# Differential attention: gates as token-major products joined to the head output, q's norm in the exponentials' scale, the rotation moved off GpSimd

## The chip, the cores and the metric

The kernel runs on one core of one Trainium2 chip. The metric is the time of one execution on the device in microseconds; the median over repeated runs is compared. TensorE (PE in the profile) does the matrix products and the transposes, VectorE (DVE) and ScalarE (ACT) work on their results, GpSimd (POOL) does small arithmetic, and SyncE (SP) issues most of the DMAs.

## The reference

The network has four layers (differential attention, latent attention, a gated linear recurrence, differential attention again) with a per-layer embedding gate after each, and then a second part with a state space mixer and a dilated attention whose inputs are modulated by a vector `c`. There are 256 tokens and 2048 features, all in float32. What the change touches is the differential attention of layers 0 and 3, and when the modulation's weights are fetched:

```python
def diff_attention(xn, positions, w_in, q_gain, k_gain, ..., sub_gain, w_out, layer_idx):
    u = xn @ w_in
    q, k, v, gate = jnp.split(u, 4, axis=-1)
    q = rope(rms_norm(q.reshape(B, S, H, 2, d), q_gain), positions)
    k = rope(rms_norm(k.reshape(B, S, H, 2, d), k_gain), positions)
    ...
        sc = jnp.einsum('bqhcd,bkhcd->bhcqk', q[:, s:e], k[:, :e]) * scale
        pr = jax.nn.softmax(masked(sc), axis=-1)
        w = pr[:, :, 0] - lam * pr[:, :, 1]
        return jnp.einsum('bhqk,bkhe->bqhe', w, v[:, :e])
    o = rms_norm(o, sub_gain) * (1.0 - lam_init)
    y = o.reshape(B, S, DA_WIDTH) * jax.nn.silu(gate)
    return y @ w_out
```

There are 8 heads; each has two q and two k of 128 features and a v of 256. The modulation is `silu(c) @ ada_w + ada_b`, for two later layers.

## The kernel before

Every large product is made from split operands. A weight piece of four row tiles (128 rows each) by 512 columns is fetched by SyncE into one of three buffers (`load`, L282). `split` then makes from each half of it, two row tiles, a rounded copy `hi` on ScalarE (L294) and the rest `lo` on VectorE (L296), each in one of three buffers. TensorE multiplies hi by hi, hi by lo and lo by hi and adds the three. `matB` (L328) gives feature-major results: the weights are stationary, 256 tokens are streamed, 12 products for each row tile. `matA` (L350) gives token-major results: the activations are stationary, 512 weight columns are streamed, 6 products for each row tile.

Work beside that main stream is written as generators, called jobs. `ktick` counts the row tiles of the main stream, and a job that has yielded a number goes on after so many of them. The framework then orders the instructions of each engine by priority; `high_priority(offset=self.ahead)` in `chunks` moves a weight load and its split 150 places forward. Each engine runs its queue in order.

A differential attention layer (`layer_a`) goes through four groups of 512 features (two heads). For each group it makes k, q and v as token-major products, and then the gate of the group before as a feature-major product. The job `qk` sums squares (L701 on ScalarE, L702 on VectorE), forms the norm on GpSimd (`head_r`, L576 to L581, with the power at L425), scales by the norm (L707), and rotates with `rope_apply`: GpSimd multiplies by the cosines (L565), VectorE multiplies two halves by the sines (L568) and adds (L569). Then it transposes and copies (L720, L721). The job `head` makes the scores (L736, L739), maxima (L742), exponentials (L748, their bias from GpSimd's L744), weighs the two softmaxes (L756), transposes them (L760 to L764), multiplies by v (L767 to L769), squares (L773), forms its norm on GpSimd (L776 to L784), scales (L786), transposes again (L793) and writes the feature-major output under the gain (L796). `gated` multiplies the gate's product by the norm of the rows (L606; `norm_job` has broadcast it by transposes, L440, and a copy, L451), applies Silu (L609), multiplies by the head output (L610), and splits (L613, L614). The split results of all groups are the operands of the output product `out_proj`.

The modulation runs beside all this: `ada_setup` cuts its weights into 192 pieces of 512 KB (`aw`). Every piece is fetched by SyncE at L1224 into the tile `aw` of a pool with one buffer, and multiplied and added by VectorE (L1235); `bg_rate` says how many pieces go with each weight piece of the main stream.

## Time and profile before

| | us |
|---|---|
| median of 3 runs | 3432.39 |
| lowest and highest run | 3428.05, 3438.39 |
| span of the profiled execution | 3436.4 |
| TensorE busy | 3355.9 (98%) |
| VectorE busy | 2472.9 (72%) |
| ScalarE busy | 1728.2 (50%) |
| GpSimd busy | 422.8 (12%) |

The profile is of one execution whose span lies between the lowest and the highest run; its time is not listed apart from its span, and the runs leave only a few microseconds around it. Times in it are microseconds from the start of the span, unless marked ns. A busy share says how much an engine worked, not whether it was waited for; for that one reads a stretch of the span, who waits there, and for whom. The first differential attention runs up to 437 us, the second from 1529 to 1944 us.

### The profile page before, as it was taken

What the parts mean: (1) busy time and instruction counts of PE and PEld (TensorE: products, weight loads), DVE (VectorE), ACT (ScalarE), POOL (GpSimd) and SP (SyncE); (2) the same over time, 40 slices, a digit from 0 to 9 for tenths busy, and PEclk for the clock granted to TensorE, in tenths of its full rate; (3) what the DMA queues carried; (4) which work ended last, traced back from release to release, by engine and by line L of the source; (5) the groups of instructions that cost most, each with busy time, mean ns of one, the idle gap of its engine ahead of it and who ended that gap; (6) DMA issues with size and microseconds to landing.
All of it is one profiled execution on the core that took longest, in us unless ns stands there. A gap on an engine that the chain in (4) does not pass through costs nothing.

```text
span 3436.4 us, 59860 instructions
## 1 busy us (share of the span) xinstructions
PE 3355.9 (98%) x24624; PEld 3165.8 (92%) x24624; DVE 2472.9 (72%) x3441; ACT 1728.2 (50%) x2329; POOL 422.8 (12%) x620
## 2 busy tenths in 40 slices
PE   8999999999999999999999999999999998999997
PEld 6788899998899999997788999999999998898997
DVE  7767777766677776777677678768778867777566
ACT  5455445466645676544444544555556433334443
POOL 3212201132110000112222010000000001000002
PEclk9999999999999999999999999999999999999999
DMA  6556556643465555656565566454545764786442
GB/s 234 188 200 215 211 203 223 217 142 138 149 226 200 195 183 190 224 207 218 178 216 188 191 238 230 175 184 174 193 175 184 252 233 169 297 296 240 158 143 102
DMA packets 113826, 685.48 MB, mean 199 GB/s; under 512 B 13264, under 2 KB 13968, under 8 KB 47120
## 3 DMA queue, kind: packets, MB, share of 16 engines
q1 hardware_dynamic: 109152, 670.49, 54.6%
q10 hardware_dynamic: 4400, 11.18, 1.1%
q8 instruction: 192, 3.15, 0.4%
q14 instruction: 82, 0.67, 0.1%
HBM read 679.45 MB, written 2.16 MB: 198 GB/s over the span
## 4 chain that ended last, share of the span: by engine, by line
PE 81%; DVE 8%; issue 2%; POOL 2%; DMA 2%; ACT 1%; DVEq 0%; POOLq 0%
PE acc L328 59%; PE acc L350 11%; PE ps L328 4%; DVE lo L296 2%; DMA aw<-in_ada_w_dram 2%; POOL m L425 1%; DVE aacc L1235 1%; DVE t L568 1%; PE ps L1149 1%; PE ps L736 1%; PE ps L1551 1%; DVE m L702 0%; DVE t L569 0%; POOL m L576 0%; PE ps L986 0%
## 5 line engine op out<-in xcount | busy, mean ns | idle before, releaser
L294 ACT ACTIVATE hi<-w 128x1024 fp32r<-128x1024 f32 x1082 | 1140.5, 1055 | 1514.3 <-PE acc L328 982.8
L296 DVE TENSOR_TENSOR lo<-w,hi 128x1024 fp32r<-128x1024 f32 x1082 | 1354.6, 1257 | 551.3 <-ACT hi L294 545.0
L328 PE MATMUL acc<-x,hi 128*128 128x256 f32 x7168 | 1314.0, 285 | 8.5 <-DVE x L1425 3.6
L328 PEld LDWEIGHTS acc<-x,hi 128*128 128x128 f32 x7168 | 1121.4, 192 | 17.7 <-issue 6.2
L328 PE MATMUL acc<-x,lo 128*128 128x256 f32 x3584 | 1016.3, 284 | 0.2 <-DVE lo L296 0.2
L328 PE MATMUL acc<-s,hi 128*128 128x256 f32 x4864 | 882.5, 284 | 2.5 <-DVE t L938 2.4
L328 PEld LDWEIGHTS acc<-s,hi 128*128 128x128 f32 x4864 | 760.7, 192 | 2.9 <-issue 2.6
L328 PE MATMUL acc<-s,lo 128*128 128x256 f32 x2432 | 689.9, 284 | 0.5 <-DVE lo L296 0.5
L328 PEld LDWEIGHTS acc<-x,lo 128*128 128x128 f32 x3584 | 689.2, 192 | 1.1 <-DVE lo L296 0.4
L350 PE MATMUL acc<-hi,x 128*128 128x512 f32 x1920 | 603.2, 395 | 2.1 <-ACT hi L294 2.1
L328 PEld LDWEIGHTS acc<-s,lo 128*128 128x128 f32 x2432 | 467.9, 192 | 1.3 <-DVE lo L296 0.9
L350 PEld LDWEIGHTS acc<-hi,x 128*128 128x128 f32 x1920 | 358.8, 189 | 75.2 <-ACT hi L294 3.1
L350 PE MATMUL acc<-lo,x 128*128 128x512 f32 x960 | 381.1, 397 | 33.5 <-DVE lo L296 33.4
L1235 DVE SCALAR_TENSOR_TENSOR aacc<-aw,siluc,aacc 128x512 f32<-128x512 f32 x255 | 208.1, 816 | 146.9 <-DMA aw<-in_ada_w_dram 144.5
L350 PEld LDWEIGHTS acc<-lo,x 128*128 128x128 f32 x960 | 181.3, 189 | 87.9 <-DVE lo L296 49.8
L328 PE MATMUL ps<-x,hi 128*128 128x256 f32 (+1 forms) x576 | 107.7, 286 | 0.3 <-DVE x L1266 0.3
L328 PEld LDWEIGHTS ps<-x,hi 128*128 128x128 f32 (+1 forms) x576 | 88.5, 185 | 1.5 <-DVE x L1266 0.5
L1235 DVE SCALAR_TENSOR_TENSOR ssacc<-s,siluc,ssacc 128x512 f32<-128x512 f32 x105 | 78.7, 750 | 14.2 <-DMA s<-in_ada_w_dram 12.7
L405 POOL TENSOR_TENSOR ssacc<-ssacc,s 128x512 f32<-128x512 f32 x24 | 35.1, 1463 | 434.3 <-ACT s L399 434.2
L431 POOL TENSOR_SCALAR m<-m 128x2 f32<-128x2 f32 x16 | 13.2, 826 | 564.1 <-DVE m L415 534.0
L328 PE MATMUL ps<-x,lo 128*128 128x256 f32 (+1 forms) x288 | 81.2, 282 | 0.0
L425 POOL TENSOR_TENSOR m<-m,mhalf 128x4 f32<-128x4 f32 (+2 forms) x61 | 74.2, 1217 | 11.1 <-DVE m L1374 6.1
(362 smaller groups left out, 2983.4 us busy)
## 6 DMA issues: line engine op xcount, KB each, us to landing
w<-in_a_w_in_dram SPq DMA_DIRECT2D x127, 1024.0 KB, 4.8
w<-in_a_in_w_dram SPq DMA_DIRECT2D x80, 1024.0 KB, 4.8
aw<-in_ada_w_dram SPq DMA_DIRECT2D x136, 512.0 KB, 3.7
w<-in_ple_w_gate_dram SPq DMA_DIRECT2D x64, 1024.0 KB, 5.0
w<-in_kv_w_dram SPq DMA_DIRECT2D x48, 1024.0 KB, 4.8
w<-in_a_w_out_dram SPq DMA_DIRECT2D x32, 1024.0 KB, 4.8
w<-in_c_w_in_dram SPq DMA_DIRECT2D x32, 1024.0 KB, 4.9
w<-in_a_out_w_dram SPq DMA_DIRECT2D x32, 1024.0 KB, 4.8
```

The lines of the kernel that those rows point to most:

```text
L294: nc.scalar.activation(hi[:, :m], src, AF.Copy)
L296: nc.vector.tensor_tensor(out=lo[:, :m], in0=src, in1=hi[:, :m].bitcast(F32), op=ALU.subtract)
L328: self.nc.tensor.matmul(out=o, lhsT=a[:, c0:c1], rhs=b, start=(k == 0 and p == 0 and first), stop=(k == kts - 1 and p == 2 and last))
L350: self.nc.tensor.matmul(out=a[:, t, :n], lhsT=b[:, s], rhs=w, start=(k == 0 and p == 0), stop=(k == kts - 1 and p == 2))
L405: nc.gpsimd.tensor_tensor(out=acc, in0=acc, in1=f[:, :512], op=ALU.add)
L425: self.nc.gpsimd.tensor_tensor(out=out, in0=in_, in1=h, op=ALU.pow)
L431: self.nc.gpsimd.tensor_scalar(out=m, in0=m, scalar1=1.0 / dim, scalar2=eps, op0=ALU.mult, op1=ALU.add)
L568: nc.vector.tensor_tensor(out=out[:, :, a, :], in0=x[:, :, 1 - a, :], in1=s, op=ALU.mult)
L736: nc.tensor.matmul(out=scv[:, c, :], lhsT=Q[g][:, c0 + c, t * P:(t + 1) * P], rhs=K[g][:, c0 + c, :nk], start=True, stop=False)
L1149: nc.tensor.matmul(out=qs[b][:, T * i:T * i + T], lhsT=wv[:, i * P:(i + 1) * P], rhs=xv[:, k, :], start=(kk == 0 and p == 0 and i == 0), s ...
L1235: nc.vector.scalar_tensor_tensor(out=st["acc"], in0=w[:, i, :], scalar=c, in1=st["acc"], op0=ALU.mult, op1=ALU.add)
L1551: nc.tensor.matmul(out=po[64 * k:64 * k + 64, :], lhsT=tok[:, 0, 64 * hh:64 * hh + 64], rhs=ms[k][:, 0:T], start=True, stop=False)
```

## The change

In `layer_a` the gate of a group is now computed as a token-major product, between q and v of its own group, with Silu taken straight from the result by ScalarE under the norm of the rows (`SG`). The head output is scaled by its norm and by this gate in one instruction, transposed, and split under the gain into `Y`; `gated` and the broadcast of the row norm are no longer called here. The rotation is done on VectorE alone, from the product itself, before any norm. k is scaled by its norm after it, in a later step of the job; q is not scaled at all: its norm is part of the scale and the bias of the exponentials (`RQ`). Several steps of the jobs are cut by further `yield`s and their distances differ. `out_proj` takes its operands as the heads finish (`close`). In `ada_setup` the DMA and the allocation of its tile are traced under the same high priority as the weight loads. The changed file also drops comments, which moves line numbers.

```diff
-    def norm_job(self, acc):
+    def norm_job(self, acc, rb=True):
         st = {}
         def g():
             st["r"] = self.rms_r(acc(), D, EPS)
+            if not rb:
+                return
...
-        nj, nst = self.norm_job(acc)
-        K, Q, V, oT = {}, {}, {}, {}
+        nj, nst = self.norm_job(acc, rb=False)
+        K, Q, V, SG, RQ, Y = {}, {}, {}, {}, {}, {}
         self.bg_rate = 0.45
         def tables():
...
                 self.row_load(g[:, P:], "a_q_norm", P * j, P)
                 st["k"] = self.rope_tab(tabs[:, 0:2], g[:, :P], 0, 64)
                 st["q"] = self.rope_tab(tabs[:, 2:4], g[:, P:], 0, 64)
-        def qk(which, dst, g, a):
+                gs = self.rp.tile([P, 2], F32, name="gs", tag="gs", bufs=2)
+                nc.gpsimd.tensor_scalar(
+                    out=gs, in0=self.vec("a_sub_norm", 2 * j, 2), scalar1=1.0 - li, scalar2=0.0, op0=ALU.mult, op1=ALU.add)
+                st["gs"] = gs
+        def turned(which, a, t):
+            C, S = st[which]
+            x4 = a[:, t, :].rearrange("p (h a b) -> p h a b", h=4, a=2)
+            u, v = self.tmp(), self.tmp()
+            u4 = u.rearrange("p (h a b) -> p h a b", h=4, a=2)
+            v4 = v.rearrange("p (h a b) -> p h a b", h=4, a=2)
+            nc.vector.tensor_tensor(out=u4, in0=x4, in1=C[:, t].unsqueeze(1).to_broadcast([P, 4, 2, 64]), op=ALU.mult)
+            nc.vector.tensor_tensor(
+                out=v4, in0=x4[:, :, ::-1, :], in1=S[:, t].unsqueeze(1).to_broadcast([P, 4, 2, 64]), op=ALU.mult)
+            nc.vector.tensor_tensor(out=v, in0=v, in1=u, op=ALU.add)
+            return v
+        def qk(which, dst, g, a, wait):
             tables()
-            C, S = st[which]
...
             rq = self.head_r(ss, st["r2"], nst["r"], EPS, (2, 4))
-            qrs = []
-            for t in range(2):
-                qn = self.tmp()
-                nc.vector.tensor_tensor(
-                    out=qn.rearrange("p (h e) -> p h e", h=4), in0=a[:, t, :].rearrange("p (h e) -> p h e", h=4),
-                    in1=rq[:, t, :].unsqueeze(2).to_broadcast([P, 4, P]), op=ALU.mult)
-                qr = self.tmp()
-                self.rope_apply(
-                    qr.rearrange("p (h a b) -> p h a b", h=4, a=2), qn.rearrange("p (h a b) -> p h a b", h=4, a=2),
-                    C, S, t, 4, 64)
-                qrs.append(qr)
-            yield 20
+            if which == "q":
+                rs = self.rp.tile([P, 2, 2, 4], F32, name="rq", tag="rq", bufs=3)
+                nc.gpsimd.tensor_scalar(out=rs[:, 0], in0=rq, scalar1=scale, scalar2=0.0, op0=ALU.mult, op1=ALU.add)
+                nc.gpsimd.tensor_scalar(out=rs[:, 1], in0=rq, scalar1=-scale, scalar2=0.0, op0=ALU.mult, op1=ALU.add)
+                RQ[g] = rs
+            qrs = [turned(which, a, t) for t in range(2)]
+            if which == "k":
+                yield 3
+                for t in range(2):
+                    v = qrs[t].rearrange("p (h e) -> p h e", h=4)
+                    nc.vector.tensor_tensor(
+                        out=v, in0=v, in1=rq[:, t, :].unsqueeze(2).to_broadcast([P, 4, P]), op=ALU.mult)
+            yield wait
             d = self.slot()
             for t in range(2):
                 pt = self.ps()
...
                 nc.scalar.activation(d[:, :, t * P:(t + 1) * P], pt.rearrange("p (h e) -> p h e", h=4), AF.Copy)
             dst[g] = d
-        def head(h):
+        def head(h, pend, w1, w2):
             g, c0 = h // 2, 2 * (h % 2)
-            self.finish(*pend[g])
-            if g not in oT:
-                oT[g] = self.slot()
+            self.finish(*pend)
             vs = slice(T * (h % 2), T * (h % 2) + T)
             ws = []
             for t in range(2):
...
-                nc.gpsimd.tensor_scalar(out=nm, in0=mx, scalar1=-scale, scalar2=0.0, op0=ALU.mult, op1=ALU.add)
+                nc.gpsimd.tensor_tensor(out=nm, in0=mx, in1=RQ[g][:, 1, t, c0:c0 + 2], op=ALU.mult)
...
                 for c in range(2):
                     nc.scalar.activation(
-                        e[:, c, :], scv[:, c, :], AF.Exp, bias=nm[:, c:c + 1], scale=scale, accum_out=sm[:, c:c + 1])
+                        e[:, c, :], scv[:, c, :], AF.Exp, bias=nm[:, c:c + 1], scale=RQ[g][:, 0, t, c0 + c:c0 + c + 1],
+                        accum_out=sm[:, c:c + 1])
                 rs = self.small([P, 2])
                 nc.vector.reciprocal(rs, sm)
                 co = self.small([P, 1])
                 nc.gpsimd.tensor_tensor(out=co, in0=rs[:, 1:2], in1=sm[:, 0:1], op=ALU.mult)
                 nc.gpsimd.tensor_tensor(out=co, in0=co, in1=self.nlam[:, j:j + 1], op=ALU.mult)
-                w = e[:, 0, :]
-                nc.vector.scalar_tensor_tensor(out=w, in0=e[:, 1, :], scalar=co, in1=w, op0=ALU.mult, op1=ALU.add)
-                ws.append((w, rs))
-            yield 12
+                ws.append((e, co, rs))
+            yield 2
+            for e, co, _ in ws:
+                nc.vector.scalar_tensor_tensor(
+                    out=e[:, 0, :], in0=e[:, 1, :], scalar=co, in1=e[:, 0, :], op0=ALU.mult, op1=ALU.add)
+            yield w1
             pw = self.ps()
...
             wT = self.tmp(384)
             nc.scalar.activation(wT, pw[:, :384], AF.Copy)
-            yield 2
+            yield w2
             po = self.ps()
             nc.tensor.matmul(out=po[:, 0:T], lhsT=wT[:, 0:P], rhs=V[g][:, 0, vs], start=True, stop=True)
             nc.tensor.matmul(out=po[:, T:2 * T], lhsT=wT[:, P:2 * P], rhs=V[g][:, 0, vs], start=True, stop=False)
...
                 nc.scalar.activation(sq[:, t * T:(t + 1) * T], po[:, t * T:(t + 1) * T], AF.Square, accum_out=so[:, t:t + 1])
             r0 = self.small([P, 2])
             for t in range(2):
-                nc.gpsimd.tensor_copy(out=r0[:, t:t + 1], in_=ws[t][1][:, 0:1])
+                nc.gpsimd.tensor_copy(out=r0[:, t:t + 1], in_=ws[t][2][:, 0:1])
...
             ro = self.small([P, 2])
             self.rpow(ro, a)
             nc.gpsimd.tensor_tensor(out=ro, in0=ro, in1=r0, op=ALU.mult)
+            yield 3
             o = self.tmp()
             for t in range(2):
-                nc.vector.tensor_scalar(
-                    out=o[:, t * T:(t + 1) * T], in0=po[:, t * T:(t + 1) * T], scalar1=ro[:, t:t + 1], scalar2=None,
-                    op0=ALU.mult)
-            yield 6
+                nc.vector.scalar_tensor_tensor(
+                    out=o[:, t * T:(t + 1) * T], in0=po[:, t * T:(t + 1) * T], scalar=ro[:, t:t + 1],
+                    in1=SG[g][:, t, vs], op0=ALU.mult, op1=ALU.mult)
+            yield 3
             pt = self.ps()
             for e2 in range(2):
                 for t in range(2):
                     nc.tensor.transpose(
                         pt[:, e2 * T + t * P:e2 * T + (t + 1) * P], o[:, t * T + e2 * P:t * T + (e2 + 1) * P], self.ident)
+            if g not in Y:
+                Y[g] = (self.slot(F32R), self.slot(F32R))
+            hi, lo = Y[g]
             for e2 in range(2):
-                nc.vector.tensor_scalar(
-                    out=oT[g][:, c0 + e2, :], in0=pt[:, e2 * T:(e2 + 1) * T], scalar1=self.vec("a_sub_norm", 2 * j + e2),
-                    scalar2=1.0 - li, op0=ALU.mult, op1=ALU.mult)
-        y = []
-        pend, heads = {}, {}
-        def gate(g):
-            a = self.groupB(W, 16, 3 * D + 512 * g, x)
-            self.finish(*heads[g])
-            y.append(self.gated(a, nst["rb"], oT.pop(g)))
+                pv, gv = pt[:, e2 * T:(e2 + 1) * T], st["gs"][:, e2:e2 + 1]
+                nc.scalar.activation(hi[:, c0 + e2, :], pv, AF.Copy, scale=gv)
+                nc.vector.scalar_tensor_tensor(
+                    out=lo[:, c0 + e2, :], in0=pv, scalar=gv, in1=hi[:, c0 + e2, :].bitcast(F32),
+                    op0=ALU.mult, op1=ALU.subtract)
+        heads = {}
         for g in range(4):
-            kj = self.go(qk("k", K, g, self.matA(W, 16, D + 512 * g, 512, x)))
-            qj = self.go(qk("q", Q, g, self.matA(W, 16, 512 * g, 512, x)))
-            a = self.matA(W, 16, 2 * D + 512 * g, 512, x)
-            v = self.flat(self.slot()).rearrange("p (t n) -> p t n", t=2)
-            for t in range(2):
-                nc.scalar.activation(v[:, t, :], a[:, t, :], AF.Copy, scale=nst["r"][:, t:t + 1])
-            V[g] = v
-            pend[g] = (kj, qj)
             last = g == 3
-            heads[g] = [self.go(head(2 * g + i), 2 + i * (8 if last else 16)) for i in range(2)]
-            if g:
-                gate(g - 1)
-        gate(3)
-        return self.out_proj(self.W("a_w_out", j), 16, y, prep)
...
         def piece(layer, q, k):
             def f():
+                src = self.W("ada_w_2", layer).part(512 * q, 512, 2 * k, 2 * k + 2)
                 if self.late:
                     w = self.flat(self.slot()).rearrange("p (a n) -> p a n", a=2)
+                    nc.sync.dma_start(out=w, in_=src)
                 else:
-                    w = self.ap_.tile([P, 2, 512], F32, name="aw", tag="aw")
-                nc.sync.dma_start(
-                    out=w, in_=self.W("ada_w_2", layer).part(512 * q, 512, 2 * k, 2 * k + 2))
+                    with self.tc.high_priority(offset=self.ahead):
+                        w = self.ap_.tile([P, 2, 512], F32, name="aw", tag="aw")
+                        nc.sync.dma_start(out=w, in_=src)
```

How the order of the instructions moves, at three places. On VectorE, around the q product of the third group of the first layer; `acc` is the product, `t` temporaries, `m` the norm or sums, `s` tables, `aacc` the modulation's sum. Before:

```order
L702 TENSOR_REDUCE m<-t 128x4 x2
L1233 TENSOR_SCALAR aacc<-aw,siluc 128x512
L296 TENSOR_TENSOR lo<-w,hi 128x1024
L707 TENSOR_TENSOR t<-acc,m 128x512
L1235 SCALAR_TENSOR_TENSOR aacc<-aw,siluc,aacc 128x512
L568 TENSOR_TENSOR t<-t,s 128x4x64
L296 TENSOR_TENSOR lo<-w,hi 128x1024
L568 TENSOR_TENSOR t<-t,s 128x4x64
L707 TENSOR_TENSOR t<-acc,m 128x512
L569 TENSOR_TENSOR t<-t 128x512
```

The same engine and product after the change:

```order
L722 TENSOR_REDUCE m<-t 128x4 x2
L710 TENSOR_TENSOR t<-acc,s 128x512
L296 TENSOR_TENSOR lo<-w,hi 128x1024
L711 TENSOR_TENSOR t<-acc,s 128x512
L710 TENSOR_TENSOR t<-acc,s 128x512
L713 TENSOR_TENSOR t<-t 128x512
L296 TENSOR_TENSOR lo<-w,hi 128x1024
L711 TENSOR_TENSOR t<-acc,s 128x512
L1273 SCALAR_TENSOR_TENSOR aacc<-aw,siluc,aacc 128x512
L713 TENSOR_TENSOR t<-t 128x512
```

The two passes with the norm `m` (L707) are gone; the rotation reads the product and the tables, and the splits stand among its six passes.

On SyncE, in the middle of the first layer; `w` are weight pieces, `aw` the modulation's. Before:

```order
L282 DMA w<-in_a_w_in_dram 128x2048 x11
L1224 DMA aw<-in_ada_w_dram 128x1024
L282 DMA w<-in_a_w_in_dram 128x2048
L1224 DMA aw<-in_ada_w_dram 128x1024
L282 DMA w<-in_a_w_in_dram 128x2048
L1224 DMA aw<-in_ada_w_dram 128x1024
```

After:

```order
L282 DMA w<-in_a_w_in_dram 128x2048 x10
L1263 DMA aw<-in_ada_w_dram 128x1024
L282 DMA w<-in_a_w_in_dram 128x2048
L1263 DMA aw<-in_ada_w_dram 128x1024
L282 DMA w<-in_a_w_in_dram 128x2048
L1263 DMA aw<-in_ada_w_dram 128x1024
L282 DMA w<-in_a_w_in_dram 128x2048 x2
```

A piece still follows a weight load each time, with shifts of one load here and there; over the whole program both orders have 136 such pieces.

On ScalarE, in the last group of the first layer, before (Silu at L609, exponentials at L748 done earlier):

```order
L609 ACT_TABLE_LOAD
L609 ACTIVATE t<-t 128x512 x2
L294 ACTIVATE hi<-w 128x1024
L613 ACTIVATE s<-t 128x512 x2
L294 ACTIVATE hi<-w 128x1024
```

and after (Silu at L847, exponentials at L767):

```order
L847 ACT_TABLE_LOAD
L847 ACTIVATE s<-acc,r 128x512
L767 ACT_TABLE_LOAD
L767 ACTIVATE t,m<-ps,m,rq 128x128
L294 ACTIVATE hi<-w 128x1024
L767 ACTIVATE t,m<-ps,m,rq 128x128
L847 ACT_TABLE_LOAD
L847 ACTIVATE s<-acc,r 128x512
L294 ACTIVATE hi<-w 128x1024
L767 ACT_TABLE_LOAD
L767 ACTIVATE t,m<-ps,m,rq 128x256
```

Silu and the exponentials of the last two heads now alternate, with a table load at each turn; over the whole program the table loads on ScalarE go from 81 to 89.

## Rows read from the trace of the kernel before

**Rows 1.** Busy time in three stretches: stretch, length, engines, clock, DMA share
```profile
core 0: us, PE busy (x) PEld busy (x) DVE busy (x) ACT busy (x) POOL busy (x), PEclk, DMA share, GB/s
35.00:437.00 402.00, 386.63 (x2136) 330.53 (x2135) 290.61 (x390) 186.65 (x287) 89.30 (x160) 1.00 0.58 205
437.00:700.00 263.00, 262.86 (x2192) 262.35 (x2191) 187.63 (x228) 127.88 (x156) 37.99 (x54) 1.00 0.60 211
1546.00:1938.00 392.00, 378.94 (x2080) 322.72 (x2081) 278.51 (x358) 184.63 (x282) 83.68 (x154) 1.00 0.57 200
```

**Rows 2.** Waits of PE, 35 to 437: total, times, longest
```profile
PE acc L350 <- DVE lo L296: 14.2, 16, 2.0
```

**Rows 3.** The same, 1546 to 1938
```profile
PE acc L350 <- DVE lo L296: 12.7, 16, 1.8
PE ps L440 <- POOL r L425: 0.6, 1, 0.6
```

**Rows 4.** Timeline of PE, 160 to 172: a product that waited
```profile
164.46 0.50 PE L350 MATMUL acc<-lo,x 128*128 128x512 f32 x1 [1.61 <-DVE lo L296]
```

**Rows 5.** Timeline of DVE in that stretch: start, us, instruction, idle before
```profile
161.03 0.69 DVE L707 TENSOR_TENSOR t<-acc,m 128x512 f32<-128x512 f32 x1 [2.38 <-POOL m L581]
...
162.10 2.31 DVE L296 TENSOR_TENSOR lo<-w,hi 128x1024 fp32r<-128x1024 f32 x1
...
165.86 1.84 DVE L568 TENSOR_TENSOR t<-t,s 128x256 f32<-128x256 f32 x2
...
168.02 1.21 DVE L296 TENSOR_TENSOR lo<-w,hi 128x1024 fp32r<-128x1024 f32 x1
```

**Rows 6.** Timeline of GpSimd in that stretch
```profile
161.89 1.43 POOL L565 TENSOR_TENSOR t<-t,s 128x512 f32<-128x512 f32 x1 [0.90 <-DVE t L707]
165.48 1.61 POOL L565 TENSOR_TENSOR t<-t,s 128x512 f32<-128x512 f32 x1 [2.17 <-DVE t L707]
```

**Rows 7.** Groups of DVE, by shape: busy us, mean ns, idle before
```profile
L702 DVE TENSOR_REDUCE m<-t 128x4 f32<-128x512 f32 x32 | 20.3, 677 | 0.0
L707 DVE TENSOR_TENSOR t<-acc,m 128x512 f32<-128x512 f32 x32 | 21.9, 685 | 31.5 <-POOL m L581 31.3
L669 DVE TENSOR_TENSOR h<-h,t 128x512 f32<-128x512 f32 x32 | 21.9, 686 | 0.0
L786 DVE TENSOR_SCALAR t<-ps,m 128x256 f32<-128x256 f32 x32 | 14.0, 479 | 20.7 <-POOL m L783 20.7
L1235 DVE SCALAR_TENSOR_TENSOR aacc<-aw,siluc,aacc 128x512 f32<-128x512 f32 x255 | 208.1, 816 | 146.9 <-DMA aw<-in_ada_w_dram 144.5
```

**Rows 8.** Waits of DVE, 35 to 437
```profile
DVE aacc L1235 <- DMA aw<-in_ada_w_dram: 35.1, 18, 4.4
```

**Rows 9.** The same, 1546 to 1938
```profile
DVE aacc L1235 <- DMA aw<-in_ada_w_dram: 21.3, 16, 2.4
```

**Rows 10.** Chain of waits, in order of time: start, length, products
```profile
319.06 10.89 PE acc L350 x48
411.34 8.63 PE acc L328 x72
```

**Rows 11.** Groups of ACT and GpSimd, by shape
```profile
L294 ACT ACTIVATE hi<-w 128x1024 fp32r<-128x1024 f32 x1066 | 1127.0, 1058 | 1482.7 <-PE acc L328 982.8 <-PE acc L350 362.8 <-issue 82.4
L814 ACT ACTIVATE s<-acc,r 128x512 f32<-128x512 f32 x16 | 10.0, 675 | 0.0
L748 ACT ACTIVATE t<-ps,m 128x256 f32<-128x256 f32 x32 | 14.9, 470 | 24.2 <-POOL m L744 24.2
L748 ACT ACT_TABLE_LOAD x5 | 6.4, 1283 | 0.1
```

**Rows 12.** Timeline of GpSimd, 709 to 712
```profile
709.57 1.01 POOL L425 TENSOR_TENSOR m<-m,mhalf 128x4 f32<-128x4 f32 x1
```

**Rows 13.** Timeline of DVE, 709 to 712
```profile
709.76 1.22 DVE L296 TENSOR_TENSOR lo<-w,hi 128x1024 fp32r<-128x1024 f32 x1
```

**Rows 14.** Waits of ACT, 35 to 437
```profile
ACT t L748 <- POOL m L744: 31.1, 14, 6.1
```

More of the change, by code (lines that the diff above doesn't have):

```diff
@@ L448, in g @@
             st["r"] = self.rms_r(acc(), D, EPS)
+            if not rb:
+                return
             yield 3
-            rb = self.rp.tile([P, T], F32, name="rb", tag="rb", bufs=2)
-            self.nc.vector.tensor_copy(out=rb, in_=self.bcast_tok(st["r"]))
-            st["rb"] = rb
+            b = self.rp.tile([P, T], F32, name="rb", tag="rb", bufs=2)
+            self.nc.vector.tensor_copy(out=b, in_=self.bcast_tok(st["r"]))
+            st["rb"] = b
         wait, self.norm_wait = self.norm_wait, 8
@@ L821, in layer_a, with value, gate @@
-        gate(3)
-        return self.out_proj(self.W("a_w_out", j), 16, y, prep)
+                pv, gv = pt[:, e2 * T:(e2 + 1) * T], st["gs"][:, e2:e2 + 1]
[4 more added lines that the diff above has]
+        heads = {}
+        for g in range(4):
+            last = g == 3
+            kj = self.go(qk("k", K, g, self.matA(W, 16, D + 512 * g, 512, x), 9))
+            qj = self.go(qk("q", Q, g, self.matA(W, 16, 512 * g, 512, x), 13))
+            if last:
+                heads[g] = [self.go(head(2 * g + i, (kj, qj), 8, 8), 16 + 3 * i) for i in range(2)]
+            def value():
+                a = self.matA(W, 16, 2 * D + 512 * g, 512, x)
+                v = self.flat(self.slot()).rearrange("p (t n) -> p t n", t=2)
+                for t in range(2):
+                    nc.scalar.activation(v[:, t, :], a[:, t, :], AF.Copy, scale=nst["r"][:, t:t + 1])
+                V[g] = v
+            def gate():
+                a = self.matA(W, 16, 3 * D + 512 * g, 512, x)
+                v = self.flat(self.slot()).rearrange("p (t n) -> p t n", t=2)
+                for t in range(2):
+                    nc.scalar.activation(v[:, t, :], a[:, t, :], AF.Silu, scale=nst["r"][:, t:t + 1])
+                SG[g] = v
+            gate()
+            value()
+            if not last:
+                heads[g] = [self.go(head(2 * g + i, (kj, qj), 10, 2), 2 + i * 20) for i in range(2)]
@@ L825, in layer_b, with close @@
+        def close(i):
+            self.finish(*heads[i])
+            return Y.pop(i)
+        return self.out_proj(self.W("a_w_out", j), 16, [None] * 4, prep, close)
     def layer_b(self, layer, x, acc, prep):
```

6 lines of the change are left out of this document (3 added, 3 removed).

## The prediction

> **What bounds the kernel now.** I read the busy shares by stretch first. From 437 to 700 us, output product and what follows the first attention layer, TensorE is busy 262.86 of 263 us [rows 1]. In the two stretches of differential attention it is not: 15.4 of 402 us and 13.1 of 392 us are idle, 28.4 in all [rows 1]. The clock is 1.00 throughout (the 2.4 GHz level), so time is lost only in waits. The second view, TensorE's waits, names one releaser: L350, the token-major product, waits for `lo`, the rest of the weight split that VectorE makes at L296, 14.2 and 12.7 us in 16 waits each [rows 2, 3]. The third view, a timeline of such a wait, shows why `lo` is late. The product waits until 164.46 [rows 4]. On VectorE, L707 (k or q times its norm) sits 2.38 us idle for GpSimd's norm (L581); behind it stands a split of 2.31 us where others take 1.21 [rows 5]. That split began at 162.10 while GpSimd was in the rotation product L565, started at 161.89 [rows 6]. So the bound is the in-order queue of VectorE around each k and q; elsewhere it is TensorE's own pace.
>
> **The change part by part.** Durations are of the profiled execution (span 3436.4 us); the median of the runs is 3432.39, so the sum is scaled by 0.9988.
>
> **Gates.** Eight groups (four in each of two layers) go from feature-major products (192 of 256 columns) to token-major (96 of 512). In the chain of waits 72 of the former last 8.63 us and 48 of the latter 10.89 us [rows 10]: 0.1199 and 0.2269 each, 23.0 and 21.8 us per group. TensorE is the bound, so 8 x 1.23 = 9.9 us go. With them go from VectorE six passes per group at about 0.69 [rows 7], 33 us in all, and two transposes with a copy per layer for the row norm; the product that waited there lost 0.6 us [rows 3]. I count 1.0 us.
>
> **Rotation and norm.** A q product costs VectorE two sums at 0.677 and six passes at 0.685, if the one with swapped halves costs as much as the others (bounds: 0.685 and, if it falls into two half passes as L568 does at 0.92 each, 1.84 [rows 5, 7]; I take the first, since its source is PSUM as in L707 and GpSimd no longer runs beside it). That makes 5.5 us, and k two passes more, 6.8. None of the six waits for GpSimd; k's scaling comes three row tiles, 4.1 us, later. So both the 2.38 us wait and the doubled split leave; L707's 31.3 us of waiting in all [rows 7] is the first part.
>
> Not all of TensorE's 28.4 us comes back. From k's sums to q's, VectorE has eight splits (8 x 1.21 = 9.7), eleven passes of up to 512 columns (k's two sums, six passes and two scalings, one maximum: 7.5), seven of up to 256 (3.4), and about five of the modulation's at 0.816 (4.1) [rows 5, 7]: 24.7 us in the 21.8 that TensorE takes. Three groups in each layer have a head there, so 6 x 2.9 = 17 us, of which the splits already made hide two halves at a time. I keep 8 us idle, near the middle between nothing and 17. It returns 28.4 - 8 = 20.4.
>
> A rule of the Trainium skill speaks against this part: "SBUF — State Buffer", section "Who interferes with whom", says that a VectorE instruction with two SBUF inputs is blocked fully by a GpSimd instruction reading SBUF that began first. Row: a split beside the rotation takes 2.31 [rows 5, 6], as the rule has it; but a split that begins 0.19 us after the power L425 takes 1.22, its plain time, though L425 has 0.82 us to run [rows 12, 13]. By the rule, the 16 norms that now stand beside splits would delay each by up to the length of a power, 1.01 in that row, 16 us on VectorE; by the row, nothing.
>
> **Modulation.** The weights' DMAs are traced with priority, but their tile still has one buffer: a DMA can't begin before the piece before it is used. By the order of the queue, 107 of 136 pieces stand as far ahead of their first use, counted in splits, as before; the other 29 move by half a load or a load, a few by two, in both directions (mean 0.02). VectorE's 35.1 and 21.3 us of waits for these DMAs [rows 8, 9] stay. I take 0, between -1 and 8, the 8 being the idle time left above.
>
> **Silu and the end of a layer.** ScalarE gets 8 more table loads at 1.283 us [rows 11], 10 us on an engine busy 187 of 402 us [rows 1]. Where it matters is the last group: while its v is computed, 21.8 us, ScalarE has eight splits at 1.058, two Silu at 0.675, four loads at 1.283 and eight exponentials at 0.47 or less [rows 11], 18.7 us, and four waits for maxima, on average 31.1 / 14 = 2.2 [rows 14]: 27.5, which the two split halves ahead (5.4) about cover. The out product's rows 0 to 11 are ready; the last head's transposes stand eleven row tiles (16 us) into it and three (4.3 us) before their use. I count 1 us per layer, -2, between 0 and -16 a layer (four waits of the longest, 6.1).
>
> The page "ScalarE: Activation LUTs", section "What ACT_TABLE_LOAD costs", in the Trainium skill adds a drain of 1.38 us to each switch. The row shows 1.283 and 0.1 of idle before it [rows 11]; by the page the eight loads more would cost 21 us, still on an engine with half its time free.
>
> **Sum.** 9.9 + 1.0 + 20.4 - 2 = 29.3; 3436.4 - 29.3 = 3407.1, times 0.9988: 3403 us.
>
> **Rivals.**
> *The splits stay late, for VectorE's waits for the modulation's DMAs are what delays them.* For it: those waits (56 us) exceed L707's (31) [rows 7 to 9] and remain. Against: the waits of TensorE sit right behind L707 and L565 [rows 4 to 6], and from 437 to 700, with the same pieces, TensorE loses 0.1 us [rows 1]. Only 9.9 + 1.0 is won: 3421.
> *The modulation does begin early and all idle time goes.* For it: the edit asks for it, and VectorE gets slack. Against: the single buffer. 9.9 + 1.0 + 28.4: 3393. Outside attention it is worth nothing, since no such wait reaches TensorE there.
> *Slower: ScalarE, in order, stands before the exponentials.* Their scale now comes from GpSimd's norm and their maximum is multiplied by it; weights' first halves queue behind them. Each of 16 heads has two such waits; at 6.1 each [rows 14] they exceed the 5.4 us of splits ahead by 6.8, at most 109 us. Against: GpSimd loses the rotation that kept it busy, and TensorE hardly waits for ScalarE now. Beyond 2 us per head the gain is gone; at 3 us, 48 in all, without the tail's own 2: 3436.4 - 31.3 + 48 = 3453.
> *The edits of the modulation do nothing* is my forecast.
>
> **How the numbers follow.** Forecast 0.62, with its own range 3396 to 3413 (17 us idle left with the tail at 2, or 3 with none); splits still late 0.16; all idle gone 0.15; ScalarE 0.07. The range 3390 to 3421 leaves out ScalarE, half of the first rival and a little of the second, 0.18. This measurement can't tell changes below about 0.3%, 10 us, from none. The forecast and the third case are faster (0.77), and half of the late splits, which lies at that bound, so 0.85; its other half is same, 0.08; slower 0.07.
>
> **What would show it.** VectorE without waits for GpSimd ahead of the rotation, splits near 1.22 throughout the attention layers; TensorE's waits for `lo` at about 8 in place of 26.9 us; the gates at 0.227 a product; waits for the modulation's DMAs unchanged. Wrong would be: `lo` waits as before, or new waits for `hi` (ScalarE) above 5 us, or TensorE waiting for the first operands of the output product.

## The result, and the profile after

The changed kernel takes 3384.63 us (median of 4 runs, 3384.12 to 3385.78) beside 3435.11 us for the kernel before on the same chip (four runs; the first three, listed above, had 3432.39): ratio 0.9854, 95% interval 0.9841 to 0.9868, 50 us faster. The profiled execution has a span of 3382.1 us, 54.3 less than before. The forecast was 3403 with a range of 3390 to 3421: the right direction, and about 18 us too little.

Busy time by stretch, after; the first and the third stretch are the differential attention of layers 0 and 3 without their first 20 to 30 us (columns as in [rows 1]):

```profile
core 0: us, PE busy (x) PEld busy (x) DVE busy (x) ACT busy (x) POOL busy (x), PEclk, DMA share, GB/s
35.00:405.00 370.00, 369.89 (x1726) 306.17 (x1725) 263.99 (x354) 197.84 (x289) 69.93 (x141) 1.00 0.62 221
405.00:672.00 267.00, 266.49 (x2213) 265.56 (x2211) 187.10 (x230) 130.48 (x165) 40.78 (x65) 1.00 0.60 208
1520.00:1883.00 363.00, 362.41 (x1690) 299.50 (x1689) 250.46 (x323) 192.52 (x283) 66.84 (x133) 1.00 0.61 215
```

Of the 28.4 us that TensorE sat idle in attention [rows 1], 0.7 is left. The granted clock is 1.00 in these rows, the 2.4 GHz level. Before, the long stretches of [rows 1] read 1.00 too, but their rounding hides a fall: from 160 to 180 us, with the wait of [rows 4] in it, it was 0.91. That is some 1.8 us lost beside the wait itself, an estimate from 0.09 of 20 us.

```profile
160.00:180.00 20.00, 16.59 (x70) 13.07 (x69) 16.54 (x20) 5.60 (x7) 3.95 (x4) 0.91 0.57 200
```

TensorE's waits from 1520 to 1883 (total us, times, longest) are one line, and from 35 to 405 there is none, where [rows 2, 3] had 14.2 and 12.7 us for `lo`:

```profile
PE ps L816 <- DVE t L809: 0.6, 2, 0.3
```

The waits of VectorE from 35 to 405 answer to [rows 8]; a line on ScalarE's waits in the same stretch answers to [rows 14]:

```profile
DVE lo L296 <- ACT hi L294: 78.3, 64, 3.4
DVE aacc L1273 <- DMA aw<-in_ada_w_dram: 9.5, 8, 3.1
DVE t L809 <- POOL m L805: 5.3, 3, 2.0
...
ACT t L767 <- POOL m L763: 1.8, 1, 1.8
```

VectorE now waits for `hi`, which ScalarE makes only when TensorE gives a buffer back: it is ahead. Nothing in the rotation waits for GpSimd, the waits for the modulation's weights fell from 35.1 to 9.5 us, and those of the exponentials for GpSimd from 31.1 to 1.8.

VectorE's timeline around one k shows the new order (start, duration, instruction, idle time before it):

```profile
135.92 1.27 DVE L722 TENSOR_REDUCE m<-t 128x4 f32<-128x512 f32 x2
137.11 0.68 DVE L710 TENSOR_TENSOR t<-acc,s 128x512 f32<-128x512 f32 x1
137.71 0.68 DVE L711 TENSOR_TENSOR t<-acc,s 128x512 f32<-128x512 f32 x1
138.31 1.21 DVE L296 TENSOR_TENSOR lo<-w,hi 128x1024 fp32r<-128x1024 f32 x1
139.44 0.68 DVE L713 TENSOR_TENSOR t<-t 128x512 f32<-128x512 f32 x1
...
142.97 0.48 DVE L809 SCALAR_TENSOR_TENSOR t<-ps,m,s 128x256 f32<-128x256 f32 x1
143.60 1.23 DVE L296 TENSOR_TENSOR lo<-w,hi 128x1024 fp32r<-128x1024 f32 x1
144.74 0.48 DVE L809 SCALAR_TENSOR_TENSOR t<-ps,m,s 128x256 f32<-128x256 f32 x1
145.14 1.28 DVE L734 TENSOR_TENSOR t<-t,m 128x512 f32<-128x512 f32 x2
```

The idle 2.38 us and the split of 2.31 us of [rows 5] are gone; the splits take 1.21 to 1.23 (on average 1.22 from 35 to 405 and from 1520 to 1883). L809, the head's last step on VectorE before its transposes (L816), is done with its second half at 145.22, and TensorE issues the last three of those transposes at 145.42, without a wait:

```profile
145.42 0.49 PE L816 MATMUL ps<-ident,t 128*128 128x128 f32 x3
```

That is close, and it matters below. The step and its transposes stand three row tiles apart now (`yield 3`), six in the kernel before (`yield 6`).

### The profile page after: what moved, and what is told of

Read it like the earlier page. It is cut to its first block, busy times and chain, and to the rows that moved or that the text cites. A ratio compares the mean times of both kernels' runs of the same rounds, so it can differ in the third digit from the quotient of the medians.

```text
span 3382.1 us, 58228 instructions
## 1 busy us (share of the span) xinstructions
PE 3330.6 (98%) x23852; PEld 3124.8 (92%) x23852; DVE 2417.3 (71%) x3375; ACT 1752.0 (52%) x2353; POOL 393.9 (12%) x606
## 4 chain that ended last, share of the span: by engine, by line
PE 91%; DVE 4%; DMA 2%; issue 1%; POOL 1%; ACT 1%; DVEq 0%; SPq 0%; POOLq 0%
PE acc L328 56%; PE acc L350 24%; PE ps L328 4%; DMA aw<-in_ada_w_dram 1%; DVE lo L296 1%; PE ps L755 1%; PE ps L1185 1%; PE ps L1589 1%; DVE aacc L1273 0%; PE ps L741 0%; PE ps L1022 0%; POOL m L425 0%; DMA s<-in_pT_dram 0%; PE ps L1709 0%; PE ps L1246 0%
## 5 line engine op out<-in xcount | busy, mean ns | idle before, releaser
L328 PE MATMUL acc<-x,hi 128*128 128x256 f32 x6144 | 1125.5, 285 | 8.2 <-DVE x L1463 3.2
L328 PEld LDWEIGHTS acc<-x,hi 128*128 128x128 f32 x6144 | 960.9, 192 | 16.2 <-issue 6.2
L328 PE MATMUL acc<-x,lo 128*128 128x256 f32 x3072 | 870.6, 283 | 0.0
L350 PE MATMUL acc<-hi,x 128*128 128x512 f32 x2432 | 760.6, 394 | 1.3 <-ACT hi L294 1.3
L328 PEld LDWEIGHTS acc<-x,lo 128*128 128x128 f32 x3072 | 590.7, 192 | 0.0
L350 PEld LDWEIGHTS acc<-hi,x 128*128 128x128 f32 x2432 | 453.3, 188 | 94.4 <-ACT hi L294 1.9
L350 PE MATMUL acc<-lo,x 128*128 128x512 f32 x1216 | 476.2, 392 | 6.6 <-DVE lo L296 6.6
L350 PEld LDWEIGHTS acc<-lo,x 128*128 128x128 f32 x1216 | 229.1, 188 | 56.7 <-DVE lo L296 8.3
L425 POOL TENSOR_TENSOR m<-m,mhalf 128x4 f32<-128x4 f32 (+2 forms) x61 | 80.5, 1320 | 11.1 <-DVE m L1412 6.1
```

The source lines that it names most:

```text
L328: self.nc.tensor.matmul(out=o, lhsT=a[:, c0:c1], rhs=b, start=(k == 0 and p == 0 and first), stop=(k == kts - 1 and p == 2 and last))
L350: self.nc.tensor.matmul(out=a[:, t, :n], lhsT=b[:, s], rhs=w, start=(k == 0 and p == 0), stop=(k == kts - 1 and p == 2))
L425: self.nc.gpsimd.tensor_tensor(out=out, in0=in_, in1=h, op=ALU.pow)
```

## The experiments

Ratios are to the kernel before, timed on the same chip in each series, with 95% intervals. Old layout means the gates, gating and head output of the kernel before; new layout the token-major gates with the fused head output.

**Modulation undone, and alone.** The first kernel puts the DMAs back, the second gives them to the kernel before.

```diff
-                    with self.tc.high_priority(offset=self.ahead):
-                        w = self.ap_.tile([P, 2, 512], F32, name="aw", tag="aw")
-                        nc.sync.dma_start(out=w, in_=src)
+                    w = self.ap_.tile([P, 2, 512], F32, name="aw", tag="aw")
+                nc.sync.dma_start(out=w, in_=src)
```

> The changed kernel with one part undone: the DMAs of the modulation's weights (aw) and their tile are asked for in the ordinary order again; nothing else differs. Rotation theory (the stalls of the attention layers came from VectorE waiting for GpSimd's norm and from splits doubled beside GpSimd's rotation; the modulation is worth nothing): 3385 us, within 4 of the changed kernel, ratio to the kernel before 0.985. Modulation theory (VectorE's waits for aw fell from 56 to 20 us, and that fall is part of the gain): 3395 to 3405, ratio 0.988 to 0.991, and those waits back above 45 us.

> The kernel before with the modulation's early DMAs alone. Rotation theory: no difference from the kernel before, within 4 us, ratio 0.999 to 1.001. Modulation theory: 10 to 20 us faster, ratio 0.994 to 0.997, with VectorE's waits for aw down from 56 us to about 20.

Measured: undone 3386.64 us, 0.986 (0.9846 to 0.9874), as the changed kernel; alone 3435.99, 1.0005 (0.9996 to 1.0014). VectorE's waits for these DMAs with the edit undone, from 35 to 405 and from 1520 to 1883:

```profile
DVE aacc L1271 <- DMA aw<-in_ada_w_dram: 13.2, 9, 3.5
...
DVE aacc L1271 <- DMA aw<-in_ada_w_dram: 9.3, 7, 2.4
```

The modulation theory falls twice: the edit is worth nothing that can be told from either side, and the waits are at 22.5 us without it (20.0 with it; 28.6 and 18.7 with the edit alone). They shrank mainly because of the other parts.

**Rotation and norm alone**, in the kernel before (core of the edit; q's norm goes into the exponentials as in the change):

```diff
-                self.rope_apply(
-                    qr.rearrange("p (h a b) -> p h a b", h=4, a=2), qn.rearrange("p (h a b) -> p h a b", h=4, a=2),
-                    C, S, t, 4, 64)
-                qrs.append(qr)
-            yield 20
...
+            qrs = [turned(which, a, t) for t in range(2)]
+            if which == "k":
+                yield 3
...
+            yield 17 if which == "k" else 20
```

> The kernel before with the rotation and norm part alone: the rotation's products all on VectorE straight from the product's PSUM, k scaled three row tiles later, q's norm in the scale and bias of the exponentials; gates and head output as before. Rotation theory: nearly all of the 45 us that the starts of TensorE's products had lost come back, so 3388 to 3396, ratio 0.986 to 0.989. Gates theory (it is the 33 us of VectorE's passes that the fused gates took away which made room): only 10 to 20 us, 3415 to 3425, ratio 0.994 to 0.997. Modulation theory: 20 to 30 us, and VectorE's waits for aw stay at 56.

Measured: 3397.53 us, 0.9895 (0.988 to 0.9911), 36 us faster, just short of the rotation theory's 3388 to 3396. This kernel and the one before issue the same products in these layers, so the two can be laid side by side from the layer's first product to the output product's first. Before:

```profile
8.00:436.60 428.60, 406.17 (x2202) 344.70 (x2202) 315.21 (x427) 204.53 (x315) 103.11 (x171) 0.99 0.59 208
1529.00:1944.20 415.20, 400.87 (x2203) 341.33 (x2202) 298.22 (x387) 195.55 (x295) 93.30 (x166) 1.00 0.57 200
```

With the rotation part:

```profile
8.00:414.10 406.10, 398.86 (x2202) 344.71 (x2201) 303.42 (x419) 207.77 (x314) 82.34 (x163) 0.99 0.63 220
1507.20:1904.70 397.50, 395.12 (x2204) 343.00 (x2204) 286.11 (x380) 199.07 (x297) 74.33 (x158) 1.00 0.60 210
```

The two stretches shrink by 22.5 + 17.7 = 40.2 us. TensorE's idle time falls by 27.1 (36.8 to 9.6), and its busy time by 13.1 (807.0 to 794.0) for as many products. So the stalls cost 40 and showed as 27: the rest stood in the busy column.

**Gates, fused head output and modulation without the rotation part**: the changed kernel with the old norm and rotation put back (k and q scaled first, the cosine product on GpSimd, a fixed scale in the exponentials).

> The changed kernel with the old rotation: VectorE scales k and q by the norm first and waits for GpSimd, GpSimd makes the cosine product, the exponentials have a fixed scale; token-major gates, fused head output and early modulation stay. Rotation theory: 10 to 13 us faster than the kernel before (gates 9.9 and the row norm 1.0), 3422 to 3425, ratio 0.996 to 0.997, with splits of 2.3 us and waits for lo as before. Gates theory: 25 to 35 us faster, 3400 to 3410, ratio 0.990 to 0.993.

Measured: 3451.7 us, 1.0051 (1.0039 to 1.0064). Both theories miss: this half of the change makes the kernel slower by 18 us. Its longest waits of TensorE over the whole execution:

```profile
PE ps L816 <- DVE t L809: 36.0, 12, 4.5
PE acc L350 <- DVE lo L296: 11.2, 9, 3.0
```

The waits for `lo` fell from 33.4 us to 11.2 over the execution, but a new one of 36.0 us came, in twelve waits: the transposes of the fused head output (L816) wait for VectorE's step L809.

**What in the rotation part pays.** In the old layout, first the cosine product alone was moved off GpSimd, with the norm still first; then rotation before norm, with k and q both scaled on VectorE right behind it:

```diff
-        nc.gpsimd.tensor_tensor(out=u, in0=x, in1=c, op=ALU.mult)
+        (eng or nc.gpsimd).tensor_tensor(out=u, in0=x, in1=c, op=ALU.mult)
...
-                    C, S, t, 4, 64)
+                    C, S, t, 4, 64, nc.vector)
```

```diff
+            qrs = [turned(which, a, t) for t in range(2)]
+            for t in range(2):
+                v = qrs[t].rearrange("p (h e) -> p h e", h=4)
+                nc.vector.tensor_tensor(
+                    out=v, in0=v, in1=rq[:, t, :].unsqueeze(2).to_broadcast([P, 4, P]), op=ALU.mult)
             yield 20
```

> The kernel before, with the rotation's cosine product of the two differential layers on VectorE instead of GpSimd; the norm is still applied first, so VectorE's wait for GpSimd's norm stays, and VectorE gets 32 passes of about 0.69 us more. Shared-port theory (the doubled splits beside GpSimd's product cost most): 15 to 30 us faster than the kernel before, ratio 0.991 to 0.996, splits near 1.22. Norm-wait theory (the 2.4 us in which VectorE's queue stands still cost most): within 8 us of the kernel before, ratio 0.998 to 1.002, TensorE's waits for lo still above 20 us in the two layers.

> The kernel before with the rotation on VectorE straight from the product and both k and q scaled by their norm right behind it on VectorE, with a fixed scale in the exponentials; gates and head output as before. Order theory (it is enough that six passes stand between the sums and the first use of the norm; q's norm in the exponentials is worth nothing): 3396 to 3402, within 4 us of the run with the whole rotation part, and no wait of VectorE for GpSimd's norm. Load theory (VectorE is short of time beside k and q, so 16 passes of 0.69 us more are paid): 3405 to 3412, 8 to 12 us over the run with the whole rotation part.

Measured: 3413.91 us, 0.9929 (0.9916 to 0.9943), and 3396.69 us, 0.9885 (0.9871 to 0.9898). Off GpSimd alone gives 24 us; removing the norm's wait as well gives 15 more (6 either way); q's norm in the exponentials and k's later scaling give nothing that can be told (0.9885 against 0.9895). VectorE gets 32 passes more by the first edit, and is still busy for less time (2458.2 against 2472.9 us), because more than the splits had been slow beside GpSimd. Its groups before, from 35 to 437:

```profile
L296 DVE TENSOR_TENSOR lo<-w,hi 128x1024 fp32r<-128x1024 f32 x123 | 152.5, 1254 | 32.6 <-ACT hi L294 32.6
L568 DVE TENSOR_TENSOR t<-t,s 128x256 f32<-128x256 f32 x32 | 21.2, 688 | 0.2
L569 DVE TENSOR_TENSOR t<-t 128x512 f32<-128x512 f32 x16 | 14.2, 887 | 1.4 <-POOL t L565 1.2
```

With the cosine product on VectorE:

```profile
L296 DVE TENSOR_TENSOR lo<-w,hi 128x1024 fp32r<-128x1024 f32 x129 | 156.4, 1222 | 36.9 <-ACT hi L294 36.8
L568 DVE TENSOR_TENSOR t<-t,s 128x256 f32<-128x256 f32 x32 | 12.5, 421 | 0.0
L569 DVE TENSOR_TENSOR t<-t 128x512 f32<-128x512 f32 x16 | 11.0, 687 | 0.0
```

In this layer the rotation's own passes (L568, L569) had lost 8.7 and 3.2 us, the splits some 4. In layer 3, where L568 took 618, L569 817 and a split 1289 ns on average, they lost 6.1, 2.1 and some 9. So the 24 us are the price of GpSimd's product beside VectorE as a whole; how much of it the doubled splits are was not measured apart.

With the cosine product moved, from 35 to 420, the norm's wait stands as before and yet hardly a product waits:

```profile
PE acc L350 <- DVE lo L296: 2.0, 4, 1.0
...
DVE t L707 <- POOL m L581: 17.8, 8, 2.6
```

So in the old layout splits made ahead keep most of the 2.4 us wait from showing in TensorE's waits for `lo`; the 15 us that it still costs stand mostly elsewhere, and where was not worked out. My norm-wait theory (within 8 us of before) is refuted.

The counterpart in the changed kernel: two idle GpSimd products beside each rotation.

```diff
             qrs = [turned(which, a, t) for t in range(2)]
+            for t in range(2):
+                nc.gpsimd.tensor_tensor(
+                    out=self.tmp().rearrange("p (h a b) -> p h a b", h=4, a=2),
+                    in0=qrs[t].rearrange("p (h a b) -> p h a b", h=4, a=2),
+                    in1=st[which][0][:, t].unsqueeze(1).to_broadcast([P, 4, 2, 64]), op=ALU.mult)
```

> The changed kernel with 32 GpSimd products added, two behind each rotation, of the size and operands of the one that the change took away; nothing reads what they write, so VectorE waits for none of them. Shared-port theory: 12 to 30 us slower than the changed kernel, 3397 to 3415, ratio to the kernel before 0.989 to 0.994, with splits beside them at 2.3 us. Norm-wait theory: 3385 to 3390, ratio 0.985 to 0.987; the doubled splits are caught by the splits made ahead.

Measured: 3406.29 us, 0.9911 (0.9898 to 0.9925), some 20 us lost. VectorE waits little for the added products: 3.7 us in four waits, where its scaling of k overwrites what they read. VectorE and GpSimd in that kernel, around one k:

```profile
140.28 1.22 DVE L296 TENSOR_TENSOR lo<-w,hi 128x1024 fp32r<-128x1024 f32 x1
...
145.77 2.31 DVE L296 TENSOR_TENSOR lo<-w,hi 128x1024 fp32r<-128x1024 f32 x1
148.00 0.86 DVE L814 SCALAR_TENSOR_TENSOR t<-ps,m,s 128x256 f32<-128x256 f32 x2
```

```profile
139.91 1.64 POOL L425 TENSOR_TENSOR m<-m,mhalf 128x8 f32<-128x8 f32 x1
...
145.48 1.52 POOL L731 TENSOR_TENSOR t<-t,s 128x512 f32<-128x512 f32 x1 [1.91 <-DVE t L713]
```

The split that begins 0.29 us after GpSimd's product (L731) takes 2.31; the one that begins 0.37 us after a power (L425), which runs to 141.55, takes 1.22. L814 is the head's last step on VectorE (L809 in the changed kernel); behind the doubled split it is late, and TensorE waits 8.2 us for it in the first layer, where the changed kernel has none, and 13.8 us in eleven waits over the execution.

The Trainium skill ("SBUF — State Buffer", section "Who interferes with whom") has a VectorE instruction with two SBUF inputs blocked by any GpSimd instruction that began first and reads SBUF. The 128x512 product agrees; the power doesn't, and the 16 us that the rule would have put on the changed kernel's VectorE are not there: its splits take 1.22 us on average.

**The norm's wait in the new layout**: the changed kernel with the norm first again, all of the rotation on VectorE; and beside it the changed kernel with k and q scaled right behind the rotation and a fixed scale in the exponentials. The edit of the first:

```diff
-            qrs = [turned(which, a, t) for t in range(2)]
...
+                nc.vector.tensor_tensor(
+                    out=qn.rearrange("p (h e) -> p h e", h=4), in0=a[:, t, :].rearrange("p (h e) -> p h e", h=4),
+                    in1=rq[:, t, :].unsqueeze(2).to_broadcast([P, 4, P]), op=ALU.mult)
...
+                    C, S, t, 4, 64, nc.vector)
```

> The changed kernel with the norm applied first again (VectorE waits for GpSimd's norm before each rotation, k and q are scaled on VectorE, the exponentials have a fixed scale), but with all of the rotation on VectorE, so that no GpSimd product stands beside the splits. Additive theory (the wait is worth the 17 us that it was worth among the old gates, wherever it stands): 3398 to 3406, ratio 0.989 to 0.9915. Deadline theory (behind the fused head output the wait costs more, since that output's transposes follow three row tiles after a step queued behind it): 3408 to 3425, ratio 0.992 to 0.997, with waits of TensorE for that step above 10 us.

> The changed kernel with k and q both scaled by the norm on VectorE right behind the rotation and a fixed scale in the exponentials; the rotation stays on VectorE straight from the product. Order theory (q's norm in the exponentials and k's later scaling are worth nothing, as they were among the old gates): 3383 to 3389, ratio 0.9845 to 0.9865. Load theory (in the changed kernel VectorE's queue ahead of the fused head output is fuller, so 16 more passes of 0.68 us are paid): 3392 to 3400, ratio 0.987 to 0.9895.

Measured: norm first 3441.8 us, 1.0016 (1.0007 to 1.0025); scaled at once 3385.92, 0.9857 (0.9841 to 0.9872). The second is as the order theory has it. The first is beyond both of its theories: the deadline theory expected waits for VectorE's step above 10 us, and they are 31.0, but its 3408 to 3425 us is too low. A wait that cost about 15 us in the old layout costs some 56 in the new one. VectorE with the norm first, around one k:

```profile
141.57 1.27 DVE L723 TENSOR_REDUCE m<-t 128x4 f32<-128x512 f32 x2
...
146.03 0.69 DVE L728 TENSOR_TENSOR t<-acc,m 128x512 f32<-128x512 f32 x1 [2.53 <-POOL m L583]
...
153.11 0.75 DVE L570 TENSOR_TENSOR t<-t,s 128x256 f32<-128x256 f32 x2
153.78 0.48 DVE L809 SCALAR_TENSOR_TENSOR t<-ps,m,s 128x256 f32<-128x256 f32 x1
```

and TensorE:

```profile
151.58 0.39 PE L350 MATMUL acc<-hi,x 128*128 128x512 f32 x1
154.41 0.30 PE L816 MATMUL ps<-ident,t 128*128 128x128 f32 x1 [2.44 <-DVE t L809]
```

L809 starts 12.2 us after the sums (L723); in the changed kernel 7.1 us after them. TensorE, in order, reaches the transposes first and stops.

Not all of the 56 us is waiting, for the clock falls too. First TensorE around one of the longest waits, then layer 0 from 42 us and layer 3 from its first product, each to its last product of L350:

```profile
190.15 0.45 PE L816 MATMUL ps<-ident,t 128*128 128x128 f32 x1 [3.87 <-DVE t L809]
...
192.32 1.05 PE L350 MATMUL acc<-hi,x 128*128 128x512 f32 x2
193.17 0.63 PE L350 MATMUL acc<-lo,x 128*128 128x512 f32 x1
193.60 1.05 PE L350 MATMUL acc<-hi,x 128*128 128x512 f32 x2
```

```profile
42.00:440.80 398.80, 377.21 (x1700) 307.59 (x1699) 263.87 (x363) 192.81 (x286) 65.14 (x127) 0.97 0.58 201
1538.10:1945.30 407.20, 391.16 (x1796) 320.88 (x1796) 278.43 (x377) 202.73 (x299) 69.21 (x139) 0.99 0.59 204
```

Behind the wait of 3.87 us three products take 1.28 us from start to start, 0.427 each where the pace is 0.227: the 1.2 GHz level. A granted clock of 0.97 over 398.8 us and 0.99 over 407.2 comes to some 16 us, an estimate from rounded rows. It fits the mean clock of whole runs: 0.987 to 0.990 in the eleven of this kernel, 0.992 to 0.994 in the four of the changed one. The gates without the new rotation show the same, 0.988 to 0.989 in all five runs, so there too the clock adds to the waits.

**The deadline moved.** If the late step is the reason, later transposes must cure it. Three kernels take the same edit: gates without the new rotation, norm first on VectorE, and the changed kernel.

```diff
-            yield 3
+            yield 3 if h > 5 else 7
             pt = self.ps()
```

> The kernel of the gates without the new rotation (3451.7 us), with the fused head output's transposes seven instead of three row tiles behind VectorE's last step, in all heads but the last two. Deadline theory (that kernel was slow because those transposes, in TensorE's order, come three row tiles after a step of VectorE that stands behind the old rotation's backlog): TensorE's 36 us of waits for that step fall below 10 and the time to 3420 to 3430, ratio 0.996 to 0.999. Backlog theory (VectorE is late by itself, and any later step pays for it): within 8 us of 3450, the wait showing up at other products.

> The kernel with the norm first and all of the rotation on VectorE (3441.8 us), with the fused head output's transposes seven instead of three row tiles behind VectorE's step, in all heads but the last two. Deadline theory (the norm's wait costs 57 us there because it pushes that step past its transposes): TensorE's 31 us of waits for the step fall below 8 and the time to 3398 to 3412, near the changed kernel plus the 17 us that the wait was worth among the old gates; ratio 0.989 to 0.993. Backlog theory (VectorE is late by itself): above 3425, the waits showing up at other products.

> The changed kernel with the fused head output's transposes seven instead of three row tiles behind VectorE's step, in all heads but the last two; nothing else differs. Deadline theory (TensorE waits 3 us for that step in the changed kernel, so a later deadline has nothing to give): 3381 to 3388, ratio 0.9845 to 0.986. Backlog theory: 3 to 8 us faster than the changed kernel, 3377 to 3382, ratio 0.983 to 0.9845.

Measured: 3419.48 us, 0.9949 (0.9937 to 0.9962), from 1.0051, a little better than the deadline theory's 0.996 to 0.999; 3404.83 us, 0.991 (0.9893 to 0.9926), from 1.0016; 3385.23 us, 0.9858 (0.9843 to 0.9872), unchanged. The waits of TensorE in the first of them, over the execution:

```profile
PE acc L350 <- DVE lo L296: 14.6, 10, 3.8
PE ps L789 <- ACT t L786: 10.3, 5, 3.1
PE ps L816 <- DVE t L809: 3.6, 6, 0.7
```

Of the 36.0 us for L809, 3.6 are left; some 11 stand elsewhere now, at `lo` and L789. So the loss came from the distance of three row tiles, as the deadline theory has it, and part of it by way of the clock: the mean granted clock of the runs is 0.991 to 0.992 in the first kernel, where it was 0.988 to 0.989, and 0.993 in the second, where it was 0.987 to 0.990. With the distance widened each step of the new layout pays: old rotation 0.9949, off GpSimd 0.991, norm's wait gone 0.9858. That is 17 us (give or take 4), then 13 and 18 more (7 either way); the old layout had 24 and 15 for the last two. No variant beats the changed kernel.

## Why the prediction was wrong in its size

**The step that failed** is "Not all of TensorE's 28.4 us comes back ... I keep 8 us idle ... It returns 28.4 - 8 = 20.4". The rotation part returned 36 us by the medians (31 to 41 by the interval), 40 by the two profiles. The causes named, VectorE's wait for the norm and its slow work beside GpSimd, were right; the term was mis-sized, by two errors.

*The 8 us.* I set VectorE's 24.7 us of work beside k against 21.8 us of TensorE. After, the stretch from the sums of one k to those of its q is

```profile
135.92:161.44 25.52, 25.52 (x124) 21.22 (x123) 22.45 (x35) 13.79 (x23) 5.89 (x14) 1.00 0.57 204
```

25.52 us of TensorE, since the head's scores and transposes run in it as well as the 96 products, and 22.45 of VectorE. The overload of 2.9 us is slack of 3.1. The six such stretches last 25.5 to 27.0 us, and VectorE is busy for 19.7 to 23.7 in them. VectorE's work was sized about right; the time it has to fit was not, since TensorE's small products were left out.

*The 28.4 us.* Idle time by the busy share is not what a stall costs. A record of L350 lasts 0.39 us at a pace of 0.227 [rows 10], so about 0.16 us of each delayed start lies under the record before: in the row above, the start at 154.41 is 2.83 us after the one at 151.58, 2.60 over the pace, and 2.44 are called idle. The 16 waits of a layer hide 2.6 us so, and gaps below 0.16 us show none of their loss. The prediction also read the clock as 1.00 throughout and put all lost time down to waits; the fall to 0.91 from 160 to 180 is some 1.8 us more. Counted from start to start of the products of L350 in the two traces, the 13.1 us of the busy column are about 5.6 under the records before a wait, 5.2 in starts too little late to show as idle, and 1.7 at the lower clock; the small rest stands at the other products.

**Gates**: 9.9 + 1.0, less 2, were forecast. Put on top of the rotation part they are worth 0.0041 of the time by 0.9854 against 0.9895, 14 us with some 7 either way; by the two kernels that scale k and q at once (0.9857 against 0.9885), 10. Right within that. The pace is as assumed; a stretch of the chain of waits, after, with the end of a gate and a v in it (start, length, products) gives 28.58 / 126 = 0.2268:

```profile
180.15 28.58 PE acc L350 x126
```

What I missed is that this part, as it was written, is worth its 10 us only beside the other. I had looked for late splits alone, and not at the fused output's three row tiles between VectorE's step and the transposes; with the old rotation that distance fails in 12 of 16 heads, and with seven row tiles the part gives 17 us by itself (0.9949).

**Rotation passes**: right. I took 0.685 for the product with swapped halves:

```profile
L711 DVE TENSOR_TENSOR t<-acc,s 128x512 f32<-128x512 f32 x32 | 21.8, 681 | 0.0
```

The other bound, two half passes at 0.92, came from L568 while it ran beside GpSimd; with the cosine product moved it takes 0.42. The wait and the doubled split were both named as causes, rightly; GpSimd's product, with the splits and the rotation's own passes that it slowed, is the larger, 24 us against 15.

**Modulation**: 0 is right, as far as the two runs can tell. That its waits would stay was wrong: 56.4 us became 20.0 in the two layers, without this edit 22.5. Why a VectorE with slack finds the pieces in time more often was not tried.

**The tail and ScalarE**: TensorE lost 0.5 of 267 us where the output product of the first layer follows, so the 2 us were too much. The rival in which ScalarE stands before the exponentials failed where it could be seen: their wait for GpSimd's product with the norm is 1.8 and 3.5 us in the two layers. The rival in which all idle time goes was right about the idle time and wrong about its reason; its 3393 rested on the same 28.4.

## What to carry to other kernels

Count a stall by the starts of the products, or by the stage's length for the same products, not by the idle share: here 27 us of idle time stood for 40 of loss. Read the granted clock in short stretches as well: a stall can be followed by products at half the pace, which counts as busy time. When sizing an engine's load against TensorE, count all that TensorE does in the stretch. Where one part of a change shortens the distance between a producer and an in-order consumer and another part makes the producer earlier, price them together: here one half alone was 18 us slower, the other 36 us faster, and both 50.

## What the runs showed of the hardware

The doubling of a split beside GpSimd depends on what GpSimd runs: 2.31 us behind its 128x512 product, 1.22 behind a power of 128x8 that lasted 1.64 (GpSimd's spans are rough in this profile). It is not the splits alone: the rotation's passes of 128x256 took 0.69 and 0.62 us on average in the two layers beside that product, 0.42 without it. After a wait of 3.87 us TensorE's products came at 0.427 us each instead of 0.227; with the norm first, such falls of the clock came to some 16 us over the two layers, beside 31.0 us of waits for VectorE's step. And a price moved with the schedule: VectorE's 2.5 us wait for the norm, 16 times, cost about 15 us among the old gates, some 56 with the transposes three row tiles behind, and about 20 with seven.
